# Three edits: low weight parts of the first gate product on VectorE, last gated stores from GpSimd's queue, last row sums in groups of four, three and one

## The chip, the cores and the metric

The kernel runs on one core of one Trainium2 chip. The metric is the time of one execution on the device in microseconds, less being better. The kernel before was run three times: 2304.53, 2306.4 and 2313.29 us, median 2306.4 us. One execution was also recorded by the profiler; that one took 2304.9 us, and its span from the first instruction to the last is 2303.1 us.

Engines are named as in the profile: PE (TensorE, matrix products), DVE (VectorE), ACT (ScalarE), POOL (GpSimd) and SP (SyncE, which here issues nearly all DMAs). Each engine works through its own instructions in order; a wait at the head of one engine's list holds all that stand behind it.

## What is computed

One layer over x of 2048 tokens by 1024 channels, all in float32. Cut to what matters here:

```python
h = rmsnorm(x, norm_mix_g); proj = h @ w_in
mixed = concat(rmsnorm(s5_mixer(...)), rmsnorm(chunked_attention(...)))
x = x + mixed @ w_out
h = rmsnorm(x, norm_ffn_g)
x = x + (silu(h @ w_gate) * (h @ w_up)) @ w_down      # inner width 2816
return rmsnorm(x, norm_final_g)
```

The change lies in the last three lines: the feed-forward part and the final norm.

## The kernel before

**Products.** A float32 product is made of three faster products: each operand is split into a high part (rounded to the matmul's type) and a low part (what the rounding left), and high·high, high·low and low·high are summed in PSUM (`mm3`, line 157). `split` (line 163) does the splitting: ACT casts the high part, and POOL, or the engine given as `lo_eng`, subtracts it from the original (line 166). Names in the profile: `c` holds both parts of a weight block, `hi` and `lo` those of the activations, `hd` those of the operands of the down projection.

**Order.** PE's order is the order of the program text. The orders of DVE, ACT, POOL and SP come from a scheduler, which may move instructions past each other where no dependence forbids it.

**Gate and up phase** (`gate_up_phase`, line 1343). The tokens go in two halves `hf` of 1024, the 2816 inner features in eleven steps `f` of two blocks of 128 each. In each step there is one `Proj` for w_gate and one for w_up. A `Proj` multiplies 2×2 blocks by seven products in place of eight (Strassen–Winograd; B11, T1, T2, B21, T3, B22, T4). Its constructor loads two weight blocks (`raw`) and makes four sums `S` of them on DVE (line 1373); `product` splits one of the seven weight operands into `c` and runs 12 matmuls of 512 columns. `one` runs products B11 and T1, `two` runs T2, B21 and T3, `three` runs B22 and T4. PE's order interleaves them: `one` of a new Proj, then `three` of the Proj before it, then `two` of the new one. Results are copied from PSUM to `u` by ACT (line 1391) or added to `u` by DVE (line 1395). `gate` applies SiLU; `up` multiplies by the gate (line 1438) and stores the result to memory: as seven Strassen–Winograd operands `hq` (line 1444), or, in the second half at steps 9 and 10 (blocks 9, 10, 20, 21, `TAILF`), unchanged as `hs` (line 1440). All these stores are issued by SP.

Just ahead of this phase the output projection ends with adds `xt` on DVE (line 1117) and sums of squares `sa` on POOL (lines 1124 and 1125). Beside the first steps, helpers on SP, DVE and ACT still bring in the last activation operands of the half: loads `lo<-hc` (line 1337), casts, and subtractions on DVE.

**Down phase** (`down_phase`, line 1481). The stored operands come back in groups of three steps (`hd<-hq`, `hd<-wc`, line 1499, ten tiles used in a ring), are split, multiplied in the seven-product form and added to `acc` by DVE (line 1521). `acc` starts as the residual (`acc<-x`, line 1527). For the second half the last four blocks are done by plain products in three `TAIL` tiles of 512, 256 and 256 tokens: per tile eight outputs `acc[i]`, in two groups of four, each output 12 matmuls; DVE adds each to `acc` (line 1540).

**Final norm** (`End`, line 1543). `square` squares each finished `acc[i]` on ACT and adds the squares up: in 256-token tiles into two sums, `sa` by DVE and `sb` by POOL (line 1558). `sums` adds up over channels by matmuls against a column of ones, and `newton` (line 112) makes the reciprocal root in fourteen tiny DVE instructions. `products` spreads it over the partitions by transposes on PE (line 77), copies it to SBUF as `rs` by ACT (line 153), and multiplies: five of the eight outputs on DVE (line 1575), three, `ON_POOL`, on POOL (line 1573), these scaled by ACT beforehand (line 1566). SP stores each output (line 1576). `sums` of a tile runs behind the first group of the next tile, `products` inside its second group; the last tile's run at the very end.

## Time and profile before

| | us |
|---|---|
| median of three runs | 2306.4 |
| the profiled execution | 2304.9 |
| its span | 2303.1 |
| start of the gate and up phase's first product on PE | 985.4 |
| switch to the second half of the tokens in that phase | about 1416 to 1432 |
| first product of the down phase | 1846.2 |
| last matmul with 256 columns | 2285.4 |
| last PE instruction | 2295.0 |

Reading: a row of the timeline is start, duration, engine, line, operation, and in square brackets how long the engine had been idle before and whose instruction released it. "x8" is a run of eight like instructions given as one row. A row of the table of windows gives for each engine the busy time and the number of instructions in a stretch, and PEclk, the share of its full clock that TensorE was granted there (1.00 is full, 0.50 half). A row of waits gives engine, tile and line that waited, what it waited for, and the sum, the number and the longest of such waits. From the start of the gate and up phase to the last group of the down phase PE stands still for only a few microseconds in all; behind that come the last sums, the norm and the stores.

### The profile page before, as it was taken

The page shows a single profiled execution, that of the slowest core. Times are in us where ns is not written, and L with a number is a line of the kernel's source. Part 1 is how long each engine was busy: PE and PEld are TensorE (multiplying, and loading weights), DVE is VectorE, ACT ScalarE, POOL GpSimd, SP SyncE. Part 2 cuts the span into 40 slices and gives each one's busy share as a digit, 9 for nine tenths or more (in the row PEclk, how much of TensorE's full clock was granted, in tenths as well). Part 3 has the DMA queues.
Part 4 walks back from the last instruction along what each step waited for, and adds up shares of the span by engine and source line. Part 5 has one row for each costly group of instructions (what it writes and reads, how often), then busy time and mean ns, then how long its engine had stood idle before and what let it go on. Part 6 is the DMA issues. An engine that isn't in the chain of part 4 may idle for free.

```text
span 2303.1 us, 30454 instructions
## 1 busy us (share of the span) xinstructions
PE 2183.8 (95%) x10568; PEld 1834.1 (80%) x10568; DVE 1487.8 (65%) x2286; ACT 1001.3 (43%) x1675; POOL 1061.0 (46%) x1245
## 2 busy tenths in 40 slices
PE   8978799999997899989999999999999999999997
PEld 6667688898986788778888887888888878888886
DVE  7845555656555756676775669766645376578676
ACT  6335555555557542343333335333333343344332
POOL 3416655455660433265555554555555314445442
PEclk9989999999998999999999999999999999999998
DMA  8788766766653534754554556555433287465552
GB/s 295 260 286 265 235 210 204 207 190 193 192 137 114 178 118 163 249 165 143 167 193 157 205 190 254 195 193 167 158 96 110 76 326 265 165 228 183 201 182 74
DMA packets 216370, 437.00 MB, mean 190 GB/s; under 512 B 27352, under 2 KB 58120, under 8 KB 209112
## 3 DMA queue, kind: packets, MB, share of 16 engines
q1 hardware_dynamic: 211352, 420.89, 55.0%
q0 software_dynamic: 4864, 14.17, 1.9%
q8 instruction: 83, 1.36, 0.2%
q14 instruction: 71, 0.58, 0.1%
HBM read 294.98 MB, written 132.15 MB: 185 GB/s over the span
## 4 chain that ended last, share of the span: by engine, by line
PE 59%; DVE 3%; DMA 1%; ACT 1%; issue 1%; POOL 1%; SPq 0%; DVEq 0%; ACTq 0%; POOLq 0%
PE X L74 20%; PE ps L74 18%; PE Y L74 10%; PE big L74 6%; PE W L74 5%; DVE acc L1575 1%; DMA lo<-hc 0%; DMA x<-xt 0%; DVE xt L1117 0%; DVE lo L166 0%; DVE hd L166 0%; POOL c L166 0%; ACT hi L165 0%; POOL sa L1125 0%; DMA gl<-x 0%
## 5 line engine op out<-in xcount | busy, mean ns | idle before, releaser
L74 PE MATMUL X<-hi,c 128*128 128x512 f32 x1408 | 452.2, 392 | 7.6 <-ACT u L1391 3.5
L74 PE MATMUL ps<-hd,hd 128*128 128x512 f32 (+1 forms) x1968 | 431.7, 381 | 3.9 <-DVE hd L166 3.7
L74 PEld LDWEIGHTS ps<-hd,hd 128*128 128x128 f32 x1968 | 358.8, 190 | 75.5 <-DVE hd L166 5.1
L166 POOL TENSOR_TENSOR c<-S,c 128x512 fp32r<-128x512 f32 x176 | 253.1, 1440 | 260.7 <-ACT c L165 258.8
L74 PEld LDWEIGHTS X<-hi,c 128*128 128x128 f32 x1408 | 265.8, 189 | 65.2 <-ACT u L1391 5.1
L74 PE MATMUL X<-lo,c 128*128 128x512 f32 x704 | 275.3, 391 | 0.0
L166 POOL TENSOR_TENSOR hd<-hd 128x1536 fp32r<-128x1536 f32 (+1 forms) x46 | 159.1, 3463 | 232.0 <-ACT hd L165 218.8
L166 POOL TENSOR_TENSOR c<-raw,c 128x512 fp32r<-128x512 f32 x132 | 189.0, 1432 | 137.5 <-ACT c L165 109.1
L165 ACT CAST hd<-hd 128x1536 fp32r<-128x1536 f32 (+1 forms) x106 | 147.4, 1393 | 219.4 <-DMA hd<-hq 134.5
L74 PE MATMUL Y<-hi,c 128*128 128x512 f32 x704 | 225.5, 391 | 4.8 <-DVE u L1395 4.8
L1521 DVE TENSOR_TENSOR acc<-acc,ps 128x512 f32<-128x512 f32 x196 | 129.2, 681 | 79.5 <-PE ps L74 79.1
L74 PE MATMUL big<-m,woh 128*128 128x512 f32 x512 | 165.4, 404 | 0.6 <-DVE m L166 0.4
L165 ACT CAST c<-S 128x512 fp32r<-128x512 f32 x176 | 109.5, 622 | 116.5 <-PE Y L74 59.1
L74 PE MATMUL pf<-hi,w 128*128 128x512 f32 x416 | 150.9, 415 | 9.4 <-ACT hi L729 5.8
L74 PEld LDWEIGHTS Y<-hi,c 128*128 128x128 f32 x704 | 132.6, 188 | 33.9 <-DVE u L1395 6.3
L74 PEld LDWEIGHTS X<-lo,c 128*128 128x128 f32 x704 | 133.0, 189 | 27.7
L1391 ACT COPY u<-X 128x512 f32<-128x512 f32 x132 | 77.1, 585 | 177.5 <-PE X L74 177.5
L846 DVE CUSTOM_DVE_ANT_0 s<-sc,nb 128x640 f32<-128x640 f32 (+4 forms) x128 | 94.4, 737 | 89.4 <-PE sc L74 85.9
L605 POOL TENSOR_TENSOR st<-X,a 128x128 f32<-128x128 f32 (+2 forms) x136 | 47.4, 349 | 220.0 <-ACT X L591 157.4
L165 ACT CAST c<-raw 128x512 fp32r<-128x512 f32 x132 | 82.1, 622 | 143.1 <-PE Y L74 80.3
L166 DVE TENSOR_TENSOR hd<-hd 128x1536 fp32r<-128x1536 f32 (+1 forms) x60 | 119.3, 1990 | 31.2 <-ACT hd L165 30.5
L74 PE MATMUL Y<-lo,c 128*128 128x512 f32 x352 | 137.2, 390 | 0.0
(462 smaller groups left out, 4644.2 us busy)
## 6 DMA issues: line engine op xcount, KB each, us to landing
w<-wss SPq DMA_DIRECT2D x36, 1024.0 KB, 5.5
hq<-g SPq DMA_DIRECT2D x140, 256.0 KB, 2.1
hd<-hq SPq DMA_DIRECT2D x42, 768.0 KB, 4.5
hd<-wc SPq DMA_DIRECT2D x42, 768.0 KB, 6.0
raw<-in_w_gate SPq DMA_DIRECT2D x44, 512.0 KB, 3.7
raw<-in_w_up SPq DMA_DIRECT2D x44, 512.0 KB, 4.1
wc<-px SPq DMA_DIRECT2D x66, 256.0 KB, 3.2
wss<-w SPq DMA_DIRECT2D x12, 1024.0 KB, 5.6
```

The source lines that it names most:

```text
L74: return self.tc.keep_in_program_order(self.tc.nc.tensor.matmul(*a, **b))
L165: (hi_eng or nc.scalar).copy(hi, raw)
L166: (lo_eng or nc.gpsimd).tensor_tensor(lo, raw, f32(hi), op=ALU.subtract)
L605: eng.tensor_tensor(t[:, :, :, :n], src, ar, op=ALU.mult)
L846: nc.vector.tensor_tensor_reduce(s[:, :nk].rearrange("p (a b) -> p a b", a=nch), ps[:, :nch, :half], hd.nb[:, nk - 1 :: -1].rearrange("p ( ...
L1391: nc.scalar.copy(u[:], ps[:])
L1521: V.tensor_tensor(a, a, ps[:], op=ALU.add)
L1575: nc.vector.scalar_tensor_tensor(v, v, k.go[:, i : i + 1], self.rs[:, : self.n], op0=ALU.mult, op1=ALU.mult)
```

## The change

It has three parts.

A. `Proj` gets an argument `eng`, and for the very first gate Proj (first half, step 0) the seven low weight parts are subtracted on DVE and not on POOL.

B. At the last step (f = 10) of each half the stores of the gated result are issued by POOL's DMA queue and not by SP: seven `hq` stores in the first half, four `hs` stores in the second.

C. In the second half of the tokens all eight final products of a tile are on DVE, none on POOL, and ACT's scaling for POOL falls away; all squares are added by DVE into one sum. The last tile's outputs come in groups of four, three and one in place of four and four. There the squares of outputs 4 to 7 are no longer added to the sum but kept (two in one tile `sg`), and the ones-matmuls add them: ten in place of four, ordered by square and then by column, with a PSUM bank for each of the two columns and so two `nv` instructions in `newton`. The reciprocal roots are read by the last products straight from PSUM; the copy `rs` is left out in that tile.

```diff
 class Proj:
-    def __init__(self, hT, w, f, post):
-        self.hT, self.post = hT, post
+    def __init__(self, hT, w, f, post, eng=None):
+        self.hT, self.post, self.eng = hT, post, eng
...
-        split(k, c[:, 0], c[:, 1], raw)
+        split(k, c[:, 0], c[:, 1], raw, self.eng)
...
-            nc.sync.dma_start(S["h"][TAILF.index(f + r * F2), :, c * 512 : (c + 1) * 512], g[:])
+            (nc.gpsimd if f == F2 - 1 else nc.sync).dma_start(S["h"][TAILF.index(f + r * F2), :, c * 512 : (c + 1) * 512], g[:])
...
-            nc.sync.dma_start(S["hq"][hf, f, n], b[:])
+            (nc.gpsimd if f == F2 - 1 else nc.sync).dma_start(S["hq"][hf, f, n], b[:])
...
-        p = Proj(hT, io[w], f, post)
+        p = Proj(hT, io[w], f, post, None if hf or f or post is up else V)
...
 class End:
-    def __init__(self, hf, acc, t0, tn):
+    def __init__(self, hf, acc, t0, tn, last=False):
+        self.last, self.on_pool = last, () if hf else ON_POOL
...
-        n, m = self.n, (i + 1) % 2 if self.n <= 256 and i > 1 else 0
-        if i == 0 or i == 1 and n <= 256:
...
+        n, v = self.n, self.acc[i][:, self.ts]
+        if i == 0:
...
+        elif self.last and i > 3:
+            if i % 2 == 0:
+                self.sq = k.t(fa, "sg", [P, 512], bufs=2)
+            t = self.sq[:, i % 2 * n : i % 2 * n + n]
+            nc.scalar.activation(t, v, AF.Square)
+            self.sa.append(t)
         else:
             t = k.t(fa, "sg", [P, 512], bufs=2)
-            nc.scalar.activation(t[:, :n], self.acc[i][:, self.ts], AF.Square)
-            (nc.gpsimd if m else nc.vector).tensor_tensor(self.sa[m][:, :n], self.sa[m][:, :n], t[:, :n], op=ALU.add)
+            nc.scalar.activation(t[:, :n], v, AF.Square)
+            V.tensor_tensor(self.sa[0], self.sa[0], t[:, :n], op=ALU.add)
...
-        for i in ON_POOL:
+        for i in self.on_pool:
...
-            if i in ON_POOL:
-                nc.gpsimd.tensor_tensor(v, v, self.rs[:, : self.n], op=ALU.mult)
+            if i in self.on_pool:
+                nc.gpsimd.tensor_tensor(v, v, rs, op=ALU.mult)
...
-    for i in (0, 4):
-        down(hs, ds, range(i, i + 4), acc, t0, tn, e, last and i and last.products)
+    for i, n in ((0, 4), (4, 3), (7, 1)) if e.last else ((0, 4), (4, 4)):
+        down(hs, ds, range(i, i + n), acc, t0, tn, e, last and i == 4 and last.products)
```

In `rstd_steps` the ones-matmuls run over squares outside and columns inside where no copy is wanted (`out is None`), and the transposed roots are then handed on in PSUM.

What this does to the engines' lists is seen at three places. First DVE at the start of the gate and up phase; `raw_10590` and `raw_10591` are the first gate Proj's weights, `raw_10692` and `raw_10693` the first up Proj's, `c_…` the split operands. Before:

```order
L1117 TENSOR_TENSOR xt_10482<-xt_10482,big_10484 128x1024
L1373 TENSOR_TENSOR S_10594<-raw_10591 128x512
L1373 TENSOR_TENSOR S_10596<-S_10594,raw_10590 128x512
L1373 TENSOR_TENSOR S_10598<-raw_10590,raw_10591 128x512
L1373 TENSOR_TENSOR S_10600<-raw_10590,S_10596 128x512
L1373 TENSOR_TENSOR S_10696<-raw_10693 128x512
```

The same place in the changed kernel (its lines are 7 higher here):

```order
L1124 TENSOR_TENSOR xt_10482<-xt_10482,big_10484 128x1024
L1380 TENSOR_TENSOR S_10594<-raw_10591 128x512
L173 TENSOR_TENSOR c_10604<-raw_10590,c_10604 128x512
L1380 TENSOR_TENSOR S_10596<-S_10594,raw_10590 128x512
L1380 TENSOR_TENSOR S_10598<-raw_10590,raw_10591 128x512
L1380 TENSOR_TENSOR S_10600<-raw_10590,S_10596 128x512
L173 TENSOR_TENSOR c_10621<-S_10594,c_10621 128x512
L173 TENSOR_TENSOR c_10637<-S_10596,c_10637 128x512
L173 TENSOR_TENSOR c_10654<-raw_10590,c_10654 128x512
L173 TENSOR_TENSOR c_10672<-S_10598,c_10672 128x512
L1380 TENSOR_TENSOR S_10696<-raw_10693 128x512
```

Five of the seven subtractions now stand among DVE's first ten instructions of the phase, the first of them (`c_10604`, product B11) behind one sum; the other two come later, among the subtractions of `lo`.

Second, SP at the end of the second half's gate and up phase, where the down phase's first loads are issued. Before:

```order
L1440 DMA hs_74<-g_17050 128x512
L1499 DMA hd_17278<-hq_76 128x3x512
L1499 DMA hd_17282<-wc_77 128x3x512
L1499 DMA hd_17338<-hq_76 128x3x512
L1499 DMA hd_17342<-wc_77 128x3x512
L1440 DMA hs_74<-g_17070 128x512
L1440 DMA hs_74<-g_17134 128x512
L1440 DMA hs_74<-g_17151 128x512
L1527 DMA acc_3334_17286<-x_5_67 128x512
```

In the changed kernel:

```order
L1506 DMA hd_17278<-hq_76 128x3x512
L1506 DMA hd_17282<-wc_77 128x3x512
L1506 DMA hd_17338<-hq_76 128x3x512
L1506 DMA hd_17342<-wc_77 128x3x512
L1534 DMA acc_3334_17286<-x_5_67 128x512
```

The four stores, the first of which stood ahead of the loads, are gone from SP's list; eight `acc` loads and then the next pair of `hd` loads follow in both. The stores stand on POOL's list behind its last weight split of the phase. In the first half POOL's list has the seven stores between its splits, five of them in a row:

```order
L173 TENSOR_TENSOR c_14132<-raw_14118,c_14132 128x512
L173 TENSOR_TENSOR c_14149<-S_14122,c_14149 128x512
L1451 DMA hq_76<-g_13816 128x512
L1451 DMA hq_76<-g_14026 128x512
L1451 DMA hq_76<-g_14027 128x512
L1451 DMA hq_76<-g_13799 128x512
L1451 DMA hq_76<-g_14051 128x512
L173 TENSOR_TENSOR c_14164<-S_13973,c_14164 128x512
```

`c_14164` is a weight operand of the second half's first gate Proj; its subtraction now stands behind five stores, each of which waits for DVE to make its `g`.

Third, PE's end in the changed kernel, behind the last output's products (`ps_20322` is output 7; `ps_20338` and `ps_20337` are the two columns' sums):

```order
L74 MATMUL ps_20322<-hd_19842,hd_19846 128x256 x3
L74 MATMUL ps_20338<-ones_86,sa_20219 128x1
L74 MATMUL ps_20337<-ones_86,sa_20219 128x1
L74 MATMUL ps_20338<-ones_86,sg_20315 128x1
L74 MATMUL ps_20337<-ones_86,sg_20315 128x1
L74 MATMUL ps_20338<-ones_86,sg_20315 128x1
L74 MATMUL ps_20337<-ones_86,sg_20315 128x1
L74 MATMUL ps_20338<-ones_86,sg_20320 128x1
L74 MATMUL ps_20337<-ones_86,sg_20320 128x1
L74 MATMUL ps_20338<-ones_86,sg_20320 128x1
L74 MATMUL ps_20337<-ones_86,sg_20320 128x1
L77 MATMUL ps_20368<-ident_81,no_20352 128x128 x2
```

The last pair alone needs output 7's square; before, the four ones-matmuls needed both finished sums. On PE the transposes for the tile before the last now also stand behind 18 matmuls of the second group (of three) where they stood behind 24 (of four).

More of the change, by code (lines that the diff above doesn't have):

```diff
@@ L136, in spread, with rstd_steps, add @@
         te.transpose(pb[:, i * P : (i + 1) * P], o[:, c + i : c + i + 1].to_broadcast([P, P]), k.ident[:])
-def rstd_steps(k, te, psum, pool, tag, sq, n, out, then=None, **kw):
-    nt = out.shape[-1] // P
-    ps = k.t(psum, *tag, **kw)
+def rstd_steps(k, te, psum, pool, tag, sq, n, out, then=None, nt=None, **kw):
+    nt = nt or out.shape[-1] // P
+    pss = [k.t(then or psum, *tag, **kw) if i and out is None else None for i in range(nt)]
+    pss[0] = k.t(psum, *tag, **kw)
     sqs = sq if isinstance(sq, list) else [sq]
-    for i in range(nt):
-        for m, sq in enumerate(sqs):
-            te.matmul(ps[:, i : i + 1], sq[:, i * P : (i + 1) * P], k.ones[:], start=m == 0, stop=m == len(sqs) - 1)
+    def add(i, m):
+        te.matmul((pss[i] or pss[0])[:, i : i + 1], sqs[m][:, i * P : (i + 1) * P], k.ones[:], start=m == 0, stop=m == len(sqs) - 1)
+    for a, b in ((a, b) for a in range(len(sqs)) for b in range(nt)) if out is None else ((a, b) for b in range(nt) for a in range(len(sqs))):
+        add(b, a)
     with k.tc.high_priority():
-        o = newton(k, pool, ps[:, :nt], n, nt)
+        o = newton(k, pool, [p[:, i : i + 1] for i, p in enumerate(pss)] if out is None else pss[0][:, :nt], n, nt)
     yield
@@ L152, in rstd_steps @@
         te.transpose(pb[:, i * P : (i + 1) * P], o[:, i : i + 1].to_broadcast([P, P]), k.ident[:])
-    k.nc.scalar.copy(out, pb[:, : nt * P])
-    yield
+    if out is None:
+        yield pb[:, : nt * P]
+    else:
+        k.nc.scalar.copy(out, pb[:, : nt * P])
+        yield out
 def mm3(te, out, whi, wlo, xhi, xlo, first, last, **kw):
```

17 lines of the change are left out of this document (9 added, 8 removed).

## The prediction

> **What bounds the kernel now.** I read the page's first lines, then the table of PE's waits, then the timeline around each wait, then the table of windows for the granted clock.
>
> ```profile
> PE 2183.8 (95%) x10568; PEld 1834.1 (80%) x10568; DVE 1487.8 (65%) x2286; ACT 1001.3 (43%) x1675; POOL 1061.0 (46%) x1245
> PEclk9989999999998999999999999999999999999998
> ```
>
> PE is busy for 95% of the span, and the change leaves its matmuls of 512 and 256 columns as they are. So the change can only win PE's pauses, the clock lost behind them, and the end behind the last matmul. The pauses at the places it touches:
>
> ```profile
> PE ps L74 <- DVE sa L1558: 6.4, 2, 4.5
> PE ps L74 <- DVE hd L166: 3.7, 3, 1.8
> PE X L74 <- ACT u L1391: 3.5, 2, 3.3
> PE X L74 <- POOL c L166: 3.5, 1, 3.5
> ```
>
> Together they are 17.1 us, under one per cent of the span; that is the size of what is at stake. Behind a long pause the clock falls:
>
> ```profile
> 988.77:995.60 6.83, 6.01 (x14) 4.75 (x15) 6.74 (x5) 2.77 (x6) 6.83 (x5) 0.50 0.24 85
> 995.60:1003.00 7.40, 7.40 (x34) 6.08 (x34) 5.24 (x4) 2.98 (x5) 7.32 (x6) 1.00 0.61 197
> 1003.00:1011.28 8.28, 8.28 (x37) 6.53 (x35) 4.92 (x7) 5.82 (x10) 2.64 (x2) 1.00 0.87 262
> 1432.51:1435.92 3.41, 3.41 (x9) 2.63 (x8) 3.41 (x3) 2.26 (x5) 3.10 (x2) 0.50 1.05 381
> 1866.00:1869.41 3.41, 3.41 (x10) 2.63 (x9) 1.69 (x2) 2.38 (x2) 0.00 (x0) 0.50 1.05 405
> ```
>
> The columns behind the stretch's length are PE, PEld, DVE, ACT, POOL, then PEclk. Each stretch at 0.50 is 3.41 us long or twice that; 3.41 us at half clock do the work of 1.7, so each such window costs 1.7 us beside the pause that caused it.
>
> **Part A, the first gate product.**
>
> ```profile
> 986.02 0.72 DVE L1373 TENSOR_TENSOR S<-raw 128x512 f32<-128x512 f32 x1
> 986.27 1.59 POOL L1125 TENSOR_TENSOR sa<-sa,xt 128x512 f32<-128x512 f32 x1
> 987.83 1.71 POOL L166 TENSOR_TENSOR c<-raw,c 128x512 fp32r<-128x512 f32 x1
> 988.34 1.75 DVE L1373 TENSOR_TENSOR S<-raw,raw 128x512 f32<-128x512 f32 x1
> 989.59 0.80 PE L74 MATMUL X<-hi,c 128*128 128x512 f32 x1 [3.47 <-POOL c L166]
> 999.76 1.63 POOL L1125 TENSOR_TENSOR sa<-sa,xt 128x512 f32<-128x512 f32 x1
> 1006.15 0.68 DVE L1395 TENSOR_TENSOR u<-u,W 128x512 f32<-128x512 f32 x1
> 1010.82 1.90 DVE L166 TENSOR_TENSOR lo<-lo,hi 128x512 fp32r<-128x512 f32 x3 [0.52 <-ACT hi L165]
> 1013.37 0.50 PE L74 MATMUL Y<-hi,c 128*128 128x512 f32 x1 [2.09 <-DVE u L1395]
> ```
>
> PE waited until 989.59 for B11's low part. POOL could begin it only when its sum `sa` was through (987.86). On DVE it follows the sum that ends at 986.74. A DVE instruction of 512 columns takes 0.68 with POOL idle and 1.75 beside a POOL instruction; until 987.86 POOL is still busy, so I take 1.5 and put the low part's end at 988.3 and PE's restart 1.3 earlier. The seven subtractions at 0.68 are 4.8 us more for DVE; between 988.77 and 1011.28 it is idle for 0.09 + 2.16 + 3.36 = 5.6 us, and its sums there get shorter while POOL no longer works beside them. Those two things hide the added work; if they did not, it would be paid in full (see the rivals). One of the two half-clock windows behind the pause should also go, since PE then ran almost without a gap in the first: 1.7.
>
> That is 3.0 us, but the next pause takes some back. At 1013.37 PE waits for a DVE add behind the last `lo` subtractions. Their loads stood on SP until POOL's `sa` row ended at 1001.39, and that row stood behind four low parts on POOL. Without these I put its end near 999, 2.4 us earlier, and one `px` multiplication now stands ahead of the last `lo`: restart at 1011.15, **2.2 us earlier**. This pause sets the result, whatever PE gained before it. Bounds: 0, if the `lo` loads do not come sooner, and −4.5, if the pause goes entirely (2.09 more than its shift).
>
> **Part B, first half.**
>
> ```profile
> 1427.67 0.69 DVE L1373 TENSOR_TENSOR S<-raw 128x512 f32<-128x512 f32 x1
> 1431.50 0.68 DVE L1462 TENSOR_TENSOR g<-g,g 128x512 f32<-128x512 f32 x1
> 1431.70 0.50 PE L74 MATMUL X<-hi,c 128*128 128x512 f32 x1 [3.34 <-ACT u L1391]
> L505 POOL DMA_DIRECT2D u<-us x16 | 8.8, 553 | 21.8 <-DVE us L88 21.2 <-issue 0.2 <-DVE nf L88 0.2
> ```
>
> The chain into 1431.70 is: the sum `S` on DVE, ACT's cast of it, four casts of `hi`, then ACT's copy `u`, all in ACT's order. In the changed order DVE makes this `S` one instruction sooner, ahead of the multiplication by the gate; by the length of such an instruction that is 0.6 to 0.7 us. DVE's low parts of `lo`, which come before it, stay. So **−0.7**, bounds +1 (a wait of the stores on POOL passes on to PE) and −3.3 (the whole pause goes).
>
> The stores themselves I cost at nothing. What hides them: five stand on POOL ahead of the split of `c_14164`. The last of the five waits for the `g` of the row at 1431.50, which ends at 1432.2; with 0.55 for the issue (the last row, POOL's issues of another tensor) and 1.7 for the split, the operand is there at 1434.5. PE uses it in the fourth product from 1431.70. A product is 12 matmuls, 2.6 us by the window with 34 matmuls in 7.40, so with the half-clock window the fourth begins at 1431.7 + 3 × 2.6 + 1.7 = 1441.2. That leaves 6.7 us of cover; each microsecond past it would be PE's.
>
> **Part B, second half.**
>
> ```profile
> 1838.45 6.38 SPq L1440 DMA_DIRECT2D hs<-g  x3
> 1844.93 4.73 SPq L1527 DMA_DIRECT2D acc<-x  x8
> 1849.82 0.53 SPq L1499 DMA_DIRECT2D hd<-hq  x1
> 1841.53 0.69 DVE L1438 TENSOR_TENSOR g<-g,u 128x512 f32<-128x512 f32 x1
> 1861.02 1.75 DVE L166 TENSOR_TENSOR hd<-hd 128x1536 fp32r<-128x1536 f32 x1
> 1863.28 1.75 DVE L166 TENSOR_TENSOR hd<-hd 128x1536 fp32r<-128x1536 f32 x1
> 1865.09 0.50 PE L74 MATMUL ps<-hd,hd 128*128 128x512 f32 x1 [1.76 <-DVE hd L166]
> ```
>
> SP stood on its `hs` stores until 1844.83, then issued eight `acc` loads, and so issued the third pair of operands only from 1849.82. Their low parts came at 1861.02 and 1863.28, and PE paused 1.76 us and then ran one window at half clock. Without the stores the `acc` loads leave by about 1838, and the pair can leave as soon as a finished `g` frees its tile's predecessor (the row at 1841.53, end 1842.2): at 1842.3 and 1843.4, some 7 us sooner. DVE's order then sets the second low part's end at 1862.7 or so, where PE arrives at about 1862.3. So about 1.6 of the pause and the 1.7 of the window: **−3.3**. The first pause of the phase, ending at 1846.21, stays: DVE's order there is unchanged. Bounds: 0, if other loads in front of it are no sooner, and −4.
>
> Here a rule speaks against the gain. The Trainium skill, "TensorE: Matmul & The Clock Gate", section "Why this matters for your kernels", asks for "No PE-idle gaps >~3µs between matmul bursts": shorter gaps would then leave the clock alone, the 1.7 would fall out of this term, and the sum would be 1.7 smaller. The trace does not agree: 1.76 us of pause stand ahead of the 0.50 at 1866.00.
>
> **Part C, the end.**
>
> ```profile
> 2282.90 3.61 DVE L1575 SCALAR_TENSOR_TENSOR acc<-acc,g_final,rs 128x256 f32<-128x256 f32 x5 [1.65 <-ACT rs L153]
> 2286.44 1.40 DVE L1540 TENSOR_TENSOR acc<-acc,ps 128x256 f32<-128x256 f32 x4
> 2289.82 0.59 PE L74 MATMUL ps<-ones,sa 128*128 128x1 f32 x2 [4.46 <-DVE sa L1558]
> 2291.73 0.16 DVE L115 TENSOR_SCALAR nv<-ps 128x2 f32<-128x2 f32 x1 [1.96 <-PE ps L74]
> 2294.31 0.69 PE L77 MATMUL ps<-ident,no 128*128 128x128 f32 x2 [2.62 <-DVE no L123]
> 2295.44 3.56 DVE L1575 SCALAR_TENSOR_TENSOR acc<-acc,g_final,rs 128x256 f32<-128x256 f32 x5 [1.19 <-ACT rs L153]
> 2297.28 1.73 DVE L1575 SCALAR_TENSOR_TENSOR acc<-acc,g_final,rs 128x256 f32<-128x256 f32 x3
> 2296.24 4.31 SPq L1576 DMA_DIRECT2D out<-acc  x8
> ```
>
> Beside POOL the first three of five products take 0.9 each, alone the last two 0.42. Eight alone are 3.4 us, no more than five beside POOL's three (3.56). In the last tile but one the sums need two ones-matmuls for four, on squares that DVE alone adds; I take its products to start 1.3 sooner than 2282.90 for that, and to end at 2285.0. Four adds, 0.35 each by the row at 2286.44, end at 2286.3 or so; the last is output 7's, whose twelve matmuls ran while DVE was busy with the products. Its square (0.4 and a hand-over) is there at 2286.8, and behind the last pair of ones-matmuls (0.59 and a hand-over) comes `nv` at 2287.6, against 2291.73: the squares no longer pass through two sums, and most ones-matmuls are done before. That is 4.1. Leaving out `rs` saves 0.4 (transposes end at 2295.00, products start at 2295.44), the second `nv` costs 0.2. From the products' start SP took 0.8 + 4.31 = 5.1 to its last issue; with outputs ready every 0.42 I take 0.5 an issue, 4.8, another 0.3. Squares of the tile before on one engine, ones-matmuls and transposes shift by tenths either way. On the other side, the transposes for the tile before stand behind 18 matmuls and must wait some 1.9 us for `newton`; the later matmuls are the same, and the cover is DVE's queue, which is late anyway. If that pause brings a half-clock window, 1 to 1.7 come back. Together 4.1 + 0.4 − 0.2 + 0.3: **−4.6**, bounds −3 and −6.
>
> **Sum.** −2.2 − 0.7 − 3.3 − 4.6 = −10.8. Against the profiled execution, 2304.9, that is 2294.1. This execution lies 1.5 below the median of the runs shown and 0.4 above their fastest; as the after median may lie between, I say **2295**.
>
> **The rivals.**
>
> 1. *Only the end pays.* PE's pauses at 1013, 1431 and 1865 each have a second operand close behind the first; if that one is as late as before, A and B give 0 to −2.5, C −4 to −5: 2298.5 to 2302. For it: at 1013.37 casts, loads and subtractions end within a microsecond of each other. Against it: at 1865 the loads were held by SP alone.
>
> 2. *The pauses go entirely, with their windows.* At 1431.70 the pause and its 0.50 window (3.34 + 1.7), or in A the whole 2.09: 3 to 5 more, 2289 to 2291. Against it: DVE's row of subtractions ahead of 1427.67 is untouched.
>
> 3. *Slower: DVE becomes the bound at the first gate product.* At p us each, seven subtractions come 7p − 5.6 late at 1013, when nothing else on DVE gets shorter, and the longer pause costs one more window, 1.7; A's 2.2 are lost. The kernel is slower than before once 7p − 5.6 + 1.7 is over 8.6 (what B and C win), so from p = 1.79. Beside POOL's splits p is 1.75, just short of it. Beside POOL's longest it can be more:
>
> ```profile
> 2066.52 3.99 DVE L1558 TENSOR_TENSOR sa<-sa,sg 128x512 f32<-128x512 f32 x1
> ```
>
> At 3.99 it would be 2320. Against it: POOL loses just these seven splits, so most of DVE's work there runs alone.
>
> 4. *A window more.* A new pause near 2279 or a shifted one elsewhere meets the clock's windows: 1.7 each, inside the range.
>
> **How the numbers follow.** The forecast, 2291 to 2298.5, has 0.62; rival 1 has 0.24; rival 2 has 0.09; rival 3 has 0.03, and 0.02 are for what I do not see. The range 2289.5 to 2302 takes in rival 1 and most of rival 2, since the bounds of A and B reach that far. About 0.5%, 11.5 us, is what a measurement of this kernel can tell from no change; the line is 2294.9, just under my time. So half the forecast less a little, and rival 2, lie beyond it: faster 0.40, same 0.57, slower 0.03.
>
> **What would show it.** A: DVE's `c<-raw` ending near 988.3, PE's pause there near 2.2, one half window in place of two, the restart of 1013.37 some 2 us earlier. B: the third pair of `hd` loads issued 7 us sooner against the phase's start, the pause at 1865 gone with its window; in the first half the pause only 0.7 shorter. C: `nv` some 3 us behind the last large matmul (it was 6.4: the ones-matmul at 2289.82 had waited 4.46, so the last large one ended at 2285.36), products at 0.42 throughout, no `rs` row at the end. I am wrong if PE waits at 1013 for a subtraction of `c`, if POOL stands on a store while PE waits for a split, or if the clock shows more windows at 0.50 than before.

## The result, and the profile after

The changed kernel took 2301.8 us (median of 22 executions, 2294.84 to 2308.47), the kernel before 2311.0 us on the same chips (22 executions, 2304.53 to 2317.53). The ratio is **0.996, 95% interval 0.9951 to 0.997**: about 9.2 us faster, within the 0.5% that was named as the bound. Predicted were 10.8 us less than the profiled execution, and 2295 us with a range of 2289.5 to 2302. The time itself lies 6.8 above the forecast, and 4.6 of that is the level: the median of before rose from 2306.4 to 2311.0 with more executions. That the time still lies in the range, by 0.2, is luck; the difference of 9.2 is the sounder measure. Two single executions of the experiments below, 5851 us of before beside e5 to e8 and 4994 us of e4, were far slower than all others and are in no ratio.

The page of the changed kernel, its first line of busy times:

```profile
PE 2183.3 (95%) x10576; PEld 1834.7 (80%) x10576; DVE 1491.7 (65%) x2307; ACT 995.0 (43%) x1665; POOL 1038.6 (45%) x1234
```

PE's busy time is within 0.5 us of before, as it should be; DVE has 4 us more and POOL 22 us less. Its table of PE's waits shows where PE stood still (engine, tile and line that waited, what for; sum, number, longest):

```profile
PE Y L74 <- DVE u L1402: 6.2, 4, 2.4
PE ps L77 <- DVE no L124: 4.7, 3, 2.6
PE X L74 <- ACT u L1398: 4.0, 1, 4.0
PE X L74 <- ACT c L172: 2.8, 1, 2.8
PE ps L74 <- DVE hd L173: 2.0, 2, 1.8
PE ps L74 <- DVE sa L1572: 0.8, 1, 0.8
```

Gone are the wait for POOL's `c` (3.5) and most of the wait for `sa` (6.4 to 0.8); one of the two long waits for `hd` has gone (3.7 to 2.0). But the wait for `u` from ACT is 4.0 where it was 3.5, the waits for DVE's `u` are four with 6.2 in all where they were three with 4.8, and the transposes' wait for `no` has two new places, 2.1 together.

**The two spans may not be subtracted.** They are 2303.1 and 2300.1, 3.0 apart, though the kernels differ by 9.2. The first product of the gate and up phase, ahead of which the two kernels have the same work, began at 985.39 in one profile and at 991.48 in the other; over all profiles of this study it began between 985.4 and 995.2. So I compare stretches that begin and end at fixed places on PE:

- S1: from that product to PE's restart behind the second pause (1013.37 in before, 1016.70 in after),
- S2: from there to the restart that ends the down phase's first pause (1846.21; 1850.97),
- S3: from there to the first ones-matmul of the first `TAIL` tile (2261.50; 2263.73),
- S4: from there to the end of the span.

| us | parts of the change | S1 | S2 | S3 | S4 |
|---|---|---|---|---|---|
| before | none | 27.98 | 832.84 | 415.29 | 41.63 |
| after | A, B, C | 25.22 | 834.27 | 412.76 | 36.33 |

S1 is 2.8 shorter, S2 1.4 longer, S3 2.5 shorter and S4 5.3 shorter in this pair. One pair says little, though: a half-clock window is worth 1.7 and falls now here, now there. The experiments repeat each stretch several times with and without each part; the means over them are taken below. S1 begins behind PE's wait for the first product, so what ends this wait counts in no stretch.

### The profile page after: what moved, and what is told of

The parts are those of the page before. It is cut to its first block, busy times and chain, and to the rows that moved or that the text cites. A ratio compares the mean times of both kernels' runs of the same rounds, so it can differ in the third digit from the quotient of the medians.

```text
span 2300.1 us, 30480 instructions
## 1 busy us (share of the span) xinstructions
PE 2183.3 (95%) x10576; PEld 1834.7 (80%) x10576; DVE 1491.7 (65%) x2307; ACT 995.0 (43%) x1665; POOL 1038.6 (45%) x1234
## 3 DMA queue, kind: packets, MB, share of 16 engines
q8 instruction: 83, 1.36, 0.2%
## 5 line engine op out<-in xcount | busy, mean ns | idle before, releaser
L173 POOL TENSOR_TENSOR c<-S,c 128x512 fp32r<-128x512 f32 x172 | 244.3, 1422 | 264.2 <-ACT c L172 264.2
L74 PEld LDWEIGHTS X<-lo,c 128*128 128x128 f32 x704 | 133.2, 189 | 27.3
```

What stands on the lines that cost most here:

```text
L74: return self.tc.keep_in_program_order(self.tc.nc.tensor.matmul(*a, **b))
L173: (lo_eng or nc.gpsimd).tensor_tensor(lo, raw, f32(hi), op=ALU.subtract)
```

## The experiments

B1 stands for part B's first half (the `hq` stores), B2 for its second half (the `hs` stores). All stretches, in the same four places:

| run | parts | ratio to before, 95% | S1 | S2 | S3 | S4 |
|---|---|---|---|---|---|---|
| e1 | A | 0.9991 (0.9979 to 1.0003) | 27.26 | 835.81 | 415.29 | 40.50 |
| e2 | B1 | 1.0002 (0.9989 to 1.0014) | 27.55 | 834.28 | 417.42 | 41.60 |
| e3 | B2 | 0.9973 (0.9959 to 0.9987) | 27.34 | 832.16 | 412.91 | 41.91 |
| e4 | C | 0.9972 (0.996 to 0.9985) | 28.70 | 833.98 | 415.16 | 36.14 |
| e5 | A, B2, C | 0.9958 (0.9942 to 0.9973) | 25.29 | 832.24 | 413.04 | 36.36 |
| e6 | A, B, C again | 0.9967 (0.9951 to 0.9982) | 24.67 | 833.88 | 411.67 | 36.34 |
| e7 | five of B1's seven stores | one execution | 27.64 | 832.96 | 415.73 | 41.96 |
| e8 | C, without its grouping and kept squares | one execution | 28.56 | 834.56 | 415.27 | 37.83 |
| e9 | e5, but A for B11 only | one execution | 28.59 | 834.89 | 411.11 | 36.94 |
| e10 | e5, but A for all except B11 | one execution | 26.58 | 832.68 | 411.36 | 36.92 |
| e11 | e5, but C's products shared with POOL | one execution | 26.02 | 833.71 | 411.34 | 40.27 |
| e12 | e5, and one sum `S` on POOL | 0.9956 (0.9944 to 0.9969) | 25.86 | 834.90 | 413.29 | 36.36 |

**One part at a time (e1 to e4).** Each kernel is the one before with one part of the diff:

```diff
+        p = Proj(hT, io[w], f, post, None if hf or f or post is up else V)                      # e1, with split(..., self.eng)
+            (nc.gpsimd if f == F2 - 1 else nc.sync).dma_start(S["hq"][hf, f, n], b[:])          # e2
+            (nc.gpsimd if f == F2 - 1 else nc.sync).dma_start(S["h"][TAILF.index(f + r * F2), :, c * 512 : (c + 1) * 512], g[:])   # e3
+    for i, n in ((0, 4), (4, 3), (7, 1)) if e.last else ((0, 4), (4, 4)):                       # e4, with all of End
```

> Part A alone on the kernel before. The prediction's sum: 2.2 us less (a ratio of 0.9990), with the restart behind the second pause 25.0 us after the first pause begins, where it was 27.25. The view from the profile after (second pause tied to the first product through ACT's copy): whatever the first pause gives, 1 to 3 us, is kept, 0.9987 to 0.9996, and the second pause stays 2 to 2.5 us long. The rival, DVE as the bound: no gain or a loss, 1.000 and over, with PE waiting for a subtraction of c on DVE.

> Part B in the first half alone (seven hq stores by POOL). The prediction's sum: 0.7 us less, the pause at the switch 0.7 shorter. The view from the profile after: POOL, held by the second store until DVE has made its g, runs three splits beside DVE's nine subtractions of lo, which take some 9.5 us and not 6.6, so the pause at the switch does not shrink (3.3 to 4.0 us) and another of about 1 us follows: 1 to 2 us more in all, a ratio of 1.0004 to 1.0008.

> Part B in the second half alone (four hs stores by POOL). The prediction's sum: 3.3 us less (0.9986), the pause of 1.76 us in the down phase gone, and no window at half clock in the first 25 us of the phase. The other view: the pause goes, but the pause in front of it (1.7 us, staying) now draws the window, so one window at half clock remains and 1.8 to 2 us are won (0.9992).

> Part C alone. The prediction's sum: 4.6 us less (0.9980). The profile after: from the ones-matmuls of the first tile of 512 tokens to the end 36.4 us where it was 41.3, that is 5.0 less (0.9978). The rival, a new pause for the transposes that draws a window at half clock: 3 us less.

The times say that B2 and C each make the kernel faster, by 0.27% and 0.28%; A and B1 alone cannot be told from no change by their times. The stretches can tell more. In e1 the stretch S1 is only 0.7 shorter than in before, though the first pause has all but gone: the second pause is 4.83, longer than either view had it. That called for e9 and e10. In e2 S2 is 1.4 longer, as the second view there had it, which called for e5 and e7. In e3 the pause of 1.76 has gone but one half-clock window stays, behind the pause in front of it; that is the second view there too, with S3 −2.4 against before. In e4 S4 is 5.5 shorter.

**B1 taken out, and B1 with five stores (e5, e6, e7).** e5 is the changed kernel with one line put back; e6 is the changed kernel once more, beside it on the same chip; e7 puts only those five stores on POOL that stand in a row there.

```diff
-                        (nc.gpsimd if f == F2 - 1 else nc.sync).dma_start(S["hq"][hf, f, n], b[:])
+                        nc.sync.dma_start(S["hq"][hf, f, n], b[:])                                                       # e5, on after
-                        nc.sync.dma_start(S["hq"][hf, f, n], b[:])
+                        (nc.gpsimd if f == F2 - 1 and n not in (B11, B22) else nc.sync).dma_start(S["hq"][hf, f, n], b[:])   # e7, on before
```

> The changed kernel with part B of the first half undone (the seven hq stores back on SP). If POOL's stores push splits beside DVE's nine lo subtractions: the nine take 6.6 us and not 9.5, the pause at the switch is 3.3 to 3.4 and not 4.0, the second pause of 1.1 us behind it goes unless a clock window falls there, and the time is 1 to 2 us under the changed kernel's, a ratio to before of 0.9950 to 0.9960. The prediction's sum has it 0.7 over the changed kernel's.

> The changed kernel again, for a second profile of each stretch and for a comparison on the chip of e5. From the restart of the first product (X0) to the restart behind the second pause: 25 to 27 us where four profiles without part A have 27.3 to 28.7; nine lo subtractions 9.5 us; down phase to the last ones-matmuls as in e3; end as in e4. Ratio 0.995 to 0.997.

> The kernel before, with only five of the seven hq stores of the first half on POOL; the two whose g is made first (B11 and B22) stay on SP, so no split stands behind a waiting store until the five. If the held splits make the loss: the nine subtractions take 6.6 us again. If issuing from POOL itself slows DVE: they stay near 9.5 us.

The intervals of e5 and e6 overlap, so the times do not settle whether B1 costs anything. The traces do. The changed kernel at the switch of halves, POOL's rows of the timeline:

```profile
1417.01 0.58 POOL L1451 DMA_DIRECT2D hq<-g  x1 [3.38 <-DVE g L1445]
1417.62 1.31 POOL L173 TENSOR_TENSOR c<-S,c 128x512 fp32r<-128x512 f32 x1
1421.59 0.57 POOL L1451 DMA_DIRECT2D hq<-g  x1 [2.66 <-DVE g L1445]
1422.18 1.30 POOL L173 TENSOR_TENSOR c<-raw,c 128x512 fp32r<-128x512 f32 x1
1423.43 1.29 POOL L173 TENSOR_TENSOR c<-S,c 128x512 fp32r<-128x512 f32 x1
1424.67 1.29 POOL L173 TENSOR_TENSOR c<-raw,c 128x512 fp32r<-128x512 f32 x1
```

and DVE's and PE's rows at that place:

```profile
1420.01 0.68 DVE L173 TENSOR_TENSOR lo<-lo,hi 128x512 fp32r<-128x512 f32 x1
1420.61 0.68 DVE L1445 TENSOR_TENSOR g<-g,u 128x512 f32<-128x512 f32 x1
1421.21 9.52 DVE L173 TENSOR_TENSOR lo<-lo,hi 128x512 fp32r<-128x512 f32 x9
1435.27 0.80 PE L74 MATMUL X<-hi,c 128*128 128x512 f32 x1 [3.96 <-ACT u L1398]
1446.36 0.50 PE L74 MATMUL Y<-hi,c 128*128 128x512 f32 x1 [1.13 <-DVE u L1402]
```

POOL comes to its second store, whose `g` DVE has not made yet, and stands there for 2.66 us. When it is let go, three splits follow back to back, and they fall on DVE's row of nine `lo` subtractions. That row takes 9.52. DVE's instructions start 0.60 apart when nothing disturbs them (the first rows), so nine would be 8 × 0.60 + 0.68 = 5.48; the other 4.04 are the three splits' 3 × 1.3, within 0.2; in before one split beside the row cost 6.60 − 5.48 = 1.1. The Trainium skill, "SBUF — State Buffer", section "Who interferes with whom", says that a DVE instruction with two SBUF inputs contends with a GpSimd instruction that reads SBUF, and that their shared port pair is an exclusive lock; these numbers agree. Without the two early stores only one split falls beside the row. The same row of before (there L166), then of e7, then of e5:

```profile
1419.83 6.60 DVE L166 TENSOR_TENSOR lo<-lo,hi 128x512 fp32r<-128x512 f32 x9
```

```profile
1423.67 6.59 DVE L166 TENSOR_TENSOR lo<-lo,hi 128x512 fp32r<-128x512 f32 x9
1433.09 2.94 POOL L1444 DMA_DIRECT2D hq<-g  x5 [6.99 <-DVE g L1452]
```

```profile
1423.23 6.59 DVE L173 TENSOR_TENSOR lo<-lo,hi 128x512 fp32r<-128x512 f32 x9
1435.22 0.50 PE L74 MATMUL X<-hi,c 128*128 128x512 f32 x1 [3.63 <-ACT u L1398]
```

e2 and e6, the other two kernels with all seven stores on POOL, show 9.53 and 9.52. So the five stores in a row cost nothing (e7: S2 832.96, against 832.84), and the two ahead of them cost DVE 2.9 us just where it is late.

What PE pays for it is less, and less sure. The pause at the switch alone does not show it: it is 3.96 or 3.97 in the three kernels with all of B1 and 3.34 to 4.20 in the ten without the two early stores (before, e1, e3, e4, e5, e7 to e11). Taken with the pauses of over 0.3 just ahead of it and behind it, PE stands 6.3, 6.2 and 5.0 us there in after, e2 and e6, and 3.9 to 5.7 in the ten others, 4.4 in the mean: 1.5 more with B1. S2 over the runs says the same of the sign: with B1 (after, e2, e6; none has a half-clock window close behind the second pause) the mean is 834.1; without B1 it is 832.5 in the four runs that have no such window either (before, e3, e5, e10), and 834.6 in five that have one (e1, e4, e8, e9, e11). Like with like, **B1 costs 1.7 us**; it is 1.7 too when only runs with a single window of 3.41 at the switch are taken (after, e2; before, e5, e10). Against all nine, 833.7, it costs 0.5.

**Which subtractions of A matter (e9, e10).** Both are e5 with A cut in two: only the first product's low part on DVE, or all but that one.

```diff
-                split(k, c[:, 0], c[:, 1], raw, self.eng)
+                split(k, c[:, 0], c[:, 1], raw, self.eng if n == B11 else None)    # e9
+                split(k, c[:, 0], c[:, 1], raw, self.eng if n != B11 else None)    # e10
```

> As e5 (parts A, C and the second half of B), but of the seven low parts of the first gate product only that of B11 is on DVE; six are back on POOL, four of them ahead of its last sa adds. Time is counted from X0, the first matmul of the phase. The first pause is short as in part A (low part used 1.4 us behind X0, not 4.2). If the second pause's restart follows POOL's queue (sa behind the splits, as the prediction had it): no gain there, restart 27.3 to 28.7 us behind X0. If it follows the first product (ACT's copy u, then ACT's square, then sa): the gain is kept, 24.7 to 26.

> As e5, but B11's low part is on POOL as before and the other six are on DVE. The first pause is as before (low part used 4.2 us behind X0). If POOL's queue sets the second restart: sa ends 13 to 14 us behind X0 in place of 16 and the restart comes at 25 to 26.5. If the first product does: sa at 15 to 16, restart 27.3 or more.

e9, PE's first pause and POOL's last row of `sa`:

```profile
991.23 0.50 PE L74 MATMUL X<-hi,c 128*128 128x512 f32 x1 [1.14 <-ACT c L172]
994.30 1.22 PE L74 MATMUL X<-hi,c 128*128 128x512 f32 x2 [2.33 <-DVE c L173]
1005.05 1.73 POOL L1132 TENSOR_TENSOR sa<-sa,xt 128x512 f32<-128x512 f32 x1
```

e10, the same two and the restart behind the second pause:

```profile
987.23 0.50 PE L74 MATMUL X<-hi,c 128*128 128x512 f32 x1 [1.26 <-ACT c L172]
991.42 1.22 PE L74 MATMUL X<-hi,c 128*128 128x512 f32 x2 [3.46 <-POOL c L173]
1000.39 1.29 POOL L1132 TENSOR_TENSOR sa<-sa,xt 128x512 f32<-128x512 f32 x1
1013.81 0.50 PE L74 MATMUL Y<-hi,c 128*128 128x512 f32 x1 [1.29 <-DVE u L1402]
```

In e9 PE goes on 3.1 behind its first matmul (994.30 − 991.23) where it had been 4.2 in before (989.59 − 985.39), but POOL's `sa` row ends 15.6 behind it, nearly as late as without A (16.0), and S1 is 28.59: nothing gained. In e10 the first pause is as long as before, 4.2, but the `sa` row ends 14.5 behind the first matmul, and S1 is 26.58. So a shorter first pause alone brought nothing, and POOL's queue freed of six splits brought the larger part, 1.4 of 2.2. Each is one profile; S1 lies between 27.3 and 28.7 in the six runs without A and between 24.7 and 27.3 in the six with all of it, so e9 is inside the first and e10 inside the second. All of A gives 25.7 in the mean.

The first pause is not without effect, though. In the changed kernel POOL's queue no longer sets the `sa` rows. ACT's and POOL's rows there:

```profile
997.54 0.59 ACT L1398 COPY u<-X 128x512 f32<-128x512 f32 x1 [1.35 <-PE X L74]
998.02 1.06 ACT L1130 ACTIVATE xt<-xt 128x1024 f32<-128x1024 f32 x1
999.22 1.37 POOL L1131 TENSOR_TENSOR sa<-sa,xt 128x512 f32<-128x512 f32 x1 [5.27 <-DVE S L1380]
```

POOL stands idle for 5.27 us and begins when ACT has scaled `xt`, which this sum reads (the row names DVE's `S`, which it does not read; in all six runs with A it begins 1.2 behind the start of ACT's row). ACT's scaling stands behind its copy `u` of the first product. So with the queue free the chain starts at the first product, and there the first pause counts: e10, which keeps that pause, has its last `sa` row end at 14.5, the runs with all of A at 12.5 to 13.0.

Part A also moved two loads on SP, which the lists above do not show: with all of A the two `px` loads of this place leave some 10 us sooner, ahead of the next weight load. That this brings the gain by itself is not borne out: PE's restart follows the `sa` row by 11.5 to 12.7 in the six runs without A and by 12.2 to 14.8 in the six with it.

**What in C brings the gain (e8, e11).** e8 has C's products on DVE and the one sum, but two groups of four, no kept squares and the copy `rs`. e11 has the groups and kept squares, but three products on POOL as before, with ACT's scaling for them and the copy.

```diff
-            e = End(1, acc, t0, tn, t0 + tn == HALF)
+            e = End(1, acc, t0, tn)                          # e8: last=False
-                self.last, self.on_pool = last, () if hf else ON_POOL
+                self.last, self.on_pool = last, ON_POOL      # e11
-                rs = None if self.last else k.t(fa, "rs", [P, 512])[:, : self.n]
+                rs = k.t(fa, "rs", [P, 512])[:, : self.n]    # e11
```

> Part C cut down: all products and sums on DVE, but the last tile in groups of four and four, its squares in one sum, its roots copied to rs. From the ones-matmuls of the first tile to the end, part C as a whole has 36.1 to 36.3 us, before 41.6. If the groups of four, three and one with the kept squares make most of the gain, as the prediction has it (4.1 of 4.6 up to nv): 39 to 41. If products on DVE without POOL's contention make it: 36.5 to 38.

> As e5, but the final products of the second half are split between DVE and POOL as before (five and three, with ACT's scaling and the copy rs in every tile); groups of four, three and one and the kept squares stay. From the ones-matmuls of the first tile to the end: 36.3 us with all of part C, 37.8 with products on DVE and groups of four, 40.5 to 41.9 before. If the products on DVE make the larger share: 38.5 to 40. If the grouping does: 36.5 to 37.5.

S4 in four pieces, from rows such as those of the changed kernel below: its start to the end of the last matmul with 256 columns; from there to the last `nv`; from there to the first of the last products; from there to the end of the span.

| us | S4 | to the last large matmul | to `nv` | to the products | to the end |
|---|---|---|---|---|---|
| before | 41.63 | 23.86 | 6.37 | 3.71 | 7.69 |
| e8 | 37.83 | 22.22 | 4.99 | 3.72 | 6.90 |
| e11 | 40.27 | 24.26 | 4.33 | 3.77 | 7.91 |
| after | 36.33 | 22.94 | 2.76 | 3.54 | 7.09 |

The changed kernel's end, PE's rows:

```profile
2278.41 0.61 PE L74 MATMUL ps<-ones,sa 128*128 128x1 f32 x4 [0.80 <-DVE sa L1572]
2282.65 0.43 PE L77 MATMUL ps<-ident,no 128*128 128x128 f32 x2 [1.38 <-DVE no L124]
2287.16 0.61 PE L74 MATMUL ps<-ones,sa 128*128 128x1 f32 x4 [0.49 <-DVE acc L1547]
2287.67 1.95 PE L74 MATMUL ps<-ones,sg 128*128 128x1 f32 x16
```

and DVE's:

```profile
2283.52 3.25 DVE L1589 SCALAR_TENSOR_TENSOR acc<-acc,g_final,rs 128x256 f32<-128x256 f32 x8 [0.93 <-ACT rs L160]
2286.70 1.41 DVE L1547 TENSOR_TENSOR acc<-acc,ps 128x256 f32<-128x256 f32 x4
2289.43 0.38 DVE L116 TENSOR_SCALAR nv<-ps 128x1 f32<-128x1 f32 x2 [1.33 <-PE ps L74]
2292.97 3.22 DVE L1589 SCALAR_TENSOR_TENSOR acc<-acc,g_final,ps 128x256 f32<-128x256 f32 x8 [0.78 <-PE ps L77]
```

The last large matmul ends at 2287.16 − 0.49 = 2286.67, and `nv` comes 2.76 later. In e8, whose two rows follow, PE waits for the finished sum as before, 3.94 (it was 4.46):

```profile
2299.73 1.02 PE L74 MATMUL ps<-ones,sa 128*128 128x1 f32 x4 [3.94 <-DVE sa L1572]
2300.78 0.16 DVE L116 TENSOR_SCALAR nv<-ps 128x2 f32<-128x2 f32 x1 [1.11 <-PE ps L74]
```

Putting the products on DVE with one sum (before to e8) brings 3.8: 1.6 ahead of the last large matmul, 1.4 at `nv`, 0.8 behind. Adding the grouping and the kept squares (e8 to after) brings 1.5 more: 2.2 at `nv`, less 0.7 for the transposes, which now wait (1.38 in place of 0.66). In the other order, grouping without the products on DVE (e11) brings 1.4, and the products then 3.9; at 40.27 e11 lies above both ranges that were expected. Part of the first gain, in either order, is a half-clock window that before had at the second group of the last tile and neither e8 nor e11 had; e1, without C and without that window, had S4 at 40.50, so that part is about 1.1. Against e1 the products with one sum bring 2.7 and the grouping then 1.5; the grouping alone brings 0.2 and the products then 3.9. e8 and e11 are one profile each, and S4 lies between 36.1 and 36.9 in the seven with all of C.

**A try at a faster one (e12).** e5 keeps the long pause at the switch of halves, whose chain leads through one `S` on DVE. e12 makes this sum on POOL:

```diff
+                self.s1 = s(a21, self.a22, ALU.add, s_eng)     # s_eng = nc.gpsimd for the second half's first up Proj, else V
```

> As e5 (A, C and the second half of B), and the one sum S that opens the chain into the pause at the switch (second half, first up Proj) is made on POOL, which is idle there, and not on DVE behind its nine lo subtractions. If that place in DVE's order is what the pause waits for (S, cast, four casts, copy u): the cast behind S comes 1 to 2 us sooner and the pause is 1.5 to 2.5 us where e5 has 3.5; ratio 0.994 to 0.9955. If the weights' landing or the lo subtractions themselves set it: 3.3 or more, ratio as e5 (0.9958).

e12, PE's two pauses:

```profile
1432.21 0.50 PE L74 MATMUL X<-hi,c 128*128 128x512 f32 x1 [2.71 <-ACT u L1398]
1444.06 0.61 PE L74 MATMUL Y<-hi,c 128*128 128x512 f32 x1 [3.38 <-DVE u L1402]
```

The pause at the switch falls from 3.63 to 2.71, not to the 1.5 to 2.5 forecast, and 12 us later a pause of 3.38 for DVE's `u` comes that e5 does not have: DVE is behind (its nine `lo` subtractions take 7.69 beside POOL's `S`, 6.59 in e5), and PE only meets it elsewhere. Its time is that of e5 within the intervals. No run beat the changed kernel by more than the measurement can tell.

## Why the prediction was right, and where its terms were not

The forecast, faster by about 10.8 and within 0.5%, was right, and so was its main line: only pauses, clock windows and the end were to be won. One term, B1, had the wrong sign; B2 and C came out a little larger than forecast and make up 0.6 of the 2.4 that it cost. Measured by the stretches, each over all runs with and without the part:

| term | predicted | measured | from |
|---|---|---|---|
| A | −2.2 | −2.2 | S1: 27.96 without A (before, e2, e3, e4, e7, e8), 25.72 with all of A (e1, after, e5, e6, e11, e12) |
| B1 | −0.7 | +1.7 (+0.5 by the widest comparison) | S2, as above |
| B2 | −3.3 | −3.5 | S3: 415.7 without (before, e1, e2, e4, e7, e8), 412.2 with (the other eight) |
| C | −4.6 | −5.0 | S4: 41.5 without (before, e1, e2, e3, e7), 36.5 with all of it (after, e4, e5, e6, e9, e10, e12) |
| sum | −10.8 | −9.0 (−10.2 with B1 at +0.5) | the medians of the times differ by 9.2 |

**A: the sum and its reason held, two of its steps did not.** The step "This pause sets the result, whatever PE gained before it" is what e9 shows; e10 limits it, since once POOL's queue is free the `sa` row follows the first product. The last `sa` row was put near 999, 13.6 behind the first matmul; it ends 12.5 to 13.0 behind it in the six runs with A, and 15.0 to 16.2 in the six without. But the first pause shrank by more than the 1.3 that I gave it. The timeline of the changed kernel, DVE and PE:

```profile
991.46 1.36 DVE L173 TENSOR_TENSOR c<-raw,c 128x512 fp32r<-128x512 f32 x1 [0.94 <-ACT c L172]
991.48 0.80 PE L74 MATMUL X<-hi,c 128*128 128x512 f32 x1 [2.83 <-ACT c L172]
992.87 1.22 PE L74 MATMUL X<-hi,c 128*128 128x512 f32 x2 [0.17 <-DVE c L173]
1002.26 1.73 POOL L1132 TENSOR_TENSOR sa<-sa,xt 128x512 f32<-128x512 f32 x1
```

The low part begins at the moment at which the high part is cast, since DVE stands ready; I had DVE busy with the sum `S` until 1.3 behind the first matmul, as in the one profile that I had. PE uses it 1.39 behind its first matmul and not 4.20: 2.8 gained, and the second pause takes most of that back. The step "One of the two half-clock windows behind the pause should also go" failed: the changed kernel has both, as have the five other runs with all of A, in the table of windows (length, then PE, PEld, DVE, ACT, POOL, then PEclk):

```profile
991.40:994.80 3.40, 3.15 (x7) 2.05 (x8) 3.34 (x3) 0.82 (x3) 2.47 (x2) 0.50 1.00 310
994.80:998.20 3.40, 3.40 (x10) 2.63 (x9) 3.40 (x7) 2.04 (x5) 0.00 (x0) 0.50 0.34 131
```

There is a pause of 2.83 ahead of the first matmul too. It goes not with A but with the clock some 40 us before: it is 1.39 to 3.48 in the eight profiles that have one half-clock window there (e3 and e4 without A among them) and 0.35 to 1.26 in the six that have two, where PE comes later to the same chain of a load of `x`, ACT's scaling and ACT's cast; in all fourteen the first product begins 1.6 behind the start of that scaling. Rival 3 is out: of DVE's seven subtractions six took 0.68 to 0.69 and the first 1.36, and no wait of PE behind the first one is for them.

**B1: the sign was wrong, and this is the one term that failed outright.** The step was "DVE's low parts of `lo`, which come before it, stay". They stay in their order, but take 9.52 in place of 6.60. I had looked for the cost of "the stores themselves" only behind the five that stand in a row, where the 6.7 us of cover did suffice (e7). The two earlier stores hold POOL; its splits are not late for PE, but they are late enough to fall upon DVE. The warning at the end of the prediction, "POOL stands on a store while PE waits for a split", named the right place and the wrong waiter.

**B2: right, but for half of the window.** SP's rows of the changed kernel:

```profile
1838.37 6.12 SPq L1534 DMA_DIRECT2D acc<-x  x8
1847.18 0.37 SPq L1506 DMA_DIRECT2D hd<-hq  x1
1848.05 0.37 SPq L1506 DMA_DIRECT2D hd<-wc  x1
```

The third pair leaves 3.8 ahead of the phase's restart at 1850.97, where it left 3.6 behind it: 7.4 sooner, against 7 predicted. The pause at 1865 has gone. Its half-clock window has gone in half of the runs, and the last section shows which half. In the changed kernel it stands behind the phase's first pause, which stays:

```profile
1850.97 24.42 PE L74 MATMUL ps<-hd,hd 128*128 128x512 f32 x98 [1.77 <-DVE hd L173]
```

```profile
1851.50:1854.96 3.46, 3.46 (x10) 2.68 (x9) 2.15 (x3) 0.00 (x0) 0.00 (x0) 0.51 1.04 411
```

The mean of S3 with B2 is 413.0 in the four runs that still have a window there (after, e3, e5, e12) and 411.4 in the four that have none (e6, e9, e10, e11). So of the 1.7 that I gave the window about half came, and that half is the term that was mis-sized. With a window on both sides the gain is 415.3 − 413.0 = 2.3 (e2, with two windows there, left out), where I had 1.6 for the pause. The pause was 1.76; the other 0.6 was not traced.

**C: the size right, the reason in part not.** `nv` behind the last large matmul: 3.6 sooner, predicted 4.1. Leaving out `rs` against the second `nv`: 0.17, predicted 0.2. Products and stores: 0.6, predicted 0.3. Ahead of the last large matmul I gave nothing, and there 0.9 came in this pair: PE's wait for `sa` of the tile before fell from 1.95 to 0.80 and the window went, less the transposes' pause of 1.38 (feared: 1.9, with a window, which did not come). My text put the gain at `nv`, and so nearly all of C, on the squares and the ones-matmuls. At `nv` they do bring 2.0 to 2.2 of the 3.6 (before to e11, e8 to after); but of S4 as a whole they bring 0.2 to 1.5, and the products on DVE with one sum 2.7 to 3.9, when the window of before is left out.

**The rivals.** "Only the end pays" is out as a mechanism, since A and B2 pay 2.2 and 3.5 and all of A and B 4.0, where it had at most 2.5; of its three pauses it was right about 1431 alone. The time itself, 2301.8, lies in its stretch of 2298.5 to 2302 and not in the forecast's, but by the level and not by its reason. "The pauses go entirely" is out as well: the second pause is 2.45 in the changed kernel (it was 2.09), only sooner. For "A window more" there is no single place; windows moved from run to run in S2 and S3. Between the first product and the last large matmul the pair shown has one window fewer after the change than before: that near 2279 is gone.

**Left open.** Whether the changed kernel without B1 (e5) is faster than with it: by S2 it should be by 1.7 us, 0.07%, and the times of e5 and e6 could not show that. Why S1 in e1 shortened by only 0.7 with the first pause gone: its second restart followed the `sa` row by 14.8 us, where the thirteen other profiles have 11.5 to 13.5, and I did not find what was late.

## What to carry to other kernels

A store that is moved to a compute engine's queue holds that engine's work until its data is made; look at every store that moves, the first ones too, and ask beside which other engine's work the held work then falls, as three splits fell beside DVE's row here. Where a chain has two pauses some microseconds apart, the later one decides: trace what feeds it, which may be an engine's queue and not the instruction that the first pause waits for, and ask again what feeds it once that queue is free. With a noise of several microseconds ahead of the change, compare stretches between fixed places on PE over many profiles, not the ends of two spans.

## What the hardware showed that I had not expected

**The time ahead of the change varies by 10 us.** The gate and up phase began between 985.4 and 995.2 with the same instructions ahead of it. DVE's wait for a load near it (`xt<-in_xt`) is not what varies: it is 9.0 to 9.4 us in all fourteen profiles. What makes the difference was not tried.

**The same pause brings a half-clock window in one run and none in the next, and the place of the pause decides.** Behind 1.77 us of pause the changed kernel had 0.51 for 3.46 us (above). Behind 1.76 at the same place e6, the same kernel, had none:

```profile
1847.45 2.81 PE L74 MATMUL ps<-hd,hd 128*128 128x512 f32 x11 [1.76 <-DVE hd L173]
```

In each of the fourteen traces the clock changes only at times that are whole multiples of one length apart. In before the half-clock windows begin at 988.77, 1432.50, 1866.00 and 2279.01; the distances are 130, 127 and 121 times 3.413. So one can cut a trace along this grid. The stretch that holds the changed kernel's pause, then the two that share e6's:

```profile
1848.13:1851.54 3.41, 1.41 (x6) 0.67 (x5) 3.41 (x4) 0.00 (x0) 0.54 (x1) 1.00 1.05 408
```

```profile
1842.85:1846.26 3.41, 2.60 (x11) 1.59 (x9) 3.41 (x4) 0.87 (x1) 0.79 (x2) 1.00 1.04 401
1846.26:1849.67 3.41, 2.22 (x10) 1.83 (x11) 3.09 (x3) 0.00 (x0) 0.30 (x1) 1.00 1.05 407
```

In the changed kernel the whole pause falls into one stretch of the grid, PE is busy for 1.41 of 3.41 there, and the next stretch runs at half clock. In e6 a border of the grid cuts the pause into 0.57 and 1.19, PE is busy for 2.60 and 2.22, and the clock stays full. The eight runs with B2 fall apart in just this way: the pause lies in one stretch in the four that have the window (in e5 but for 0.07 us), and a border cuts it in the four that have none. From the start of the phase to 2270, in all traces, a stretch at full clock in which PE stood for 1.76 us or more was followed by one at half clock, with one exception (1.78 in e3); none in which it stood for 1.62 or less was.

The Trainium skill, "TensorE: Matmul & The Clock Gate", section "Why this matters for your kernels", asks for no gaps over about 3 us; e6 would fit that, the changed kernel does not. Where the grid lies differed from trace to trace, so a pause of this length is a chance of losing 1.7 us, and I had counted it as certain.
